# Experts' weights in chunks of 8 KB a partition, a fourth pair of split tiles, and two raw tiles fewer

## The chip, the cores and the metric

The kernel runs on one core of a Trainium2 chip. The metric is device time in microseconds (us), the median of several runs. TensorE (PE) does the matrix products, VectorE (DVE) and ScalarE (ACT) the elementwise work, GpSimd (POOL) the indirect transfers, and SyncE (SP) issues most loads; all of them are queues that work in order and wait for one another by semaphores.

## The reference, cut to what matters

One layer of a latent-token model: a recurrent branch and a neighbourhood-attention branch are merged, then comes an expert-choice mixture of experts, and that is where the change lies. 16 experts take 128 tokens of 1024 each, and every expert has three weight matrices of 2M float32 numbers (8 MB each).

```python
def expert_choice_moe(xn, w_router, w_gate, w_up, w_down):
    ...
    g, idx = lax.top_k(aff.transpose(0, 2, 1), cap)
    xe = xn[bidx, idx]
    hid = jax.nn.silu(jnp.einsum('becd,edf->becf', xe, w_gate)) * jnp.einsum('becd,edf->becf', xe, w_up)
    ye = jnp.einsum('becf,efd->becd', hid, w_down) * g[..., None].astype(xn.dtype)
    return jnp.zeros_like(xn).at[bidx, idx].add(ye)
```

## The kernel before, in words

**Split numbers.** To multiply float32 numbers with little loss, each operand is kept as a high part (a rounded copy, type fp32r) and a low part (the number less its high part). `mm3` (lines 185 to 189) makes one product from three matmuls: high by high (L187), high by low (L188), low by high (L189). In the expert stage the tokens are the stationary operand and the weights the moving one, so L188 is the first matmul of a chunk that needs the low part of the weights.

**The weight stream.** The class `Stream` (lines 67 to 159) brings all weights through the kernel as chunks of 1 MB, 128 partitions by 2048 numbers. A chunk passes three stations. `load` (L83 to L92) takes a free raw tile and has SP issue the transfer (L90). `split` (L101 to L125) takes a free pair of split tiles, has ACT copy the chunk to the high tile (`hi_copy`, L181) and, through `finish` (L94 to L99), has DVE subtract to get the low tile (L98); after that the raw tile is free for a further load. `take` (L141 to L150) hands a chunk to PE: it first gives back the pair of the chunk before, then loads what has a tile, then splits what has a pair. So the copy into a pair that was given back waits until PE has done the last matmul of the chunk that was in it.

**Tiles.** There are two kinds of slots, in deques served first in, first out. Pairs: `w0` and `w1` for the whole kernel, `x0` and `x1` from the merge stage on (L1092). Raw tiles: `ring0`, `ring1`, four `ring2`, five `ring3` and, when the routing is done, `sel` and `ring40`. At the end of the merge stage (L1526 to L1532) the pair `x1` is taken out of the pairs and its two tiles, `x1h` and `x1l`, serve as two raw tiles. The expert stage thus has three pairs and 15 raw tiles.

**Order of the expert stage** (`stage_experts`, L1617 to L1766). There are 24 chunks to an expert, 384 in all. For each of four column blocks `f` of the hidden layer, two chunks of the gate matrix and two of the up matrix (128 rows by 512 columns, four row blocks each, so 2 KB runs in memory); then eight chunks of the down matrix (two blocks of 128 rows by 1024 columns, 4 KB runs). A chunk is twelve matmuls of 512 columns. Among the chunks PE also transposes the hidden layer (`turn_h`, L1704), after chunks 4 and 6 of the down matrix the next expert's tokens (`turn_x`, L1672, followed on ACT by L1679 and L1681 and on DVE by L1682), and it adds up the list of the tokens of the expert after that (`expert_list`, L1641, from `one_hot`, L1631). POOL gathers tokens (L1652) and adds results to memory (L1760), both indirect.

**Start and end.** While the routing is still being computed, L1550 splits the first chunks, as many as there are pairs, but leaves their subtractions for later (`defer=True`). When the list of expert 0 is known, POOL gathers its tokens (L1686) and takes on two loads (L1687), DVE does the three subtractions left over, and SP issues a load after each (L1688 to L1690); then come `turn_x` of expert 0 and `one_hot` of expert 1. In the last expert `ahead` (L1771 to L1787) uses freed raw tiles for the final norm's weight (`fnorm`, issued by ACT) and for the rows of the sum; `stage_final` (L1789) works these off.

```python
            if self.pending:
                lo, x, hi, rslot = self.pending.popleft()
                (engine or self.lo_engine).tensor_sub(lo, x, hi)
                self.free.append(rslot)
...
        if not hold:
            self.release()
        self.held.append(i)
        self.load()
        self.split(most if i in self.parts else max(most, 1))
```

Of the kernel before, what the change touches and what calls it, by code (L numbers as in the profile page):

```python
# [22 lines left out]
D = 1024  # L23
# [5 lines left out]
NEXP = 16  # L29
DEXP = 2048  # L30
# [32 lines left out]
def raw(t, off, dims):  # L63
    return bass.AP(tensor=t.tensor, offset=t.offset + off, ap=dims)
# [109 lines left out]
class Kernel:  # L174
# [68 lines left out]
    def setup(self):  # L243
        nc, c = self.nc, self.const
        I = self.I
        self.par = c.tile([128, NPK], F32, name="par")
        nc.scalar.dma_start(self.par, I["pk"])
        self.ident = c.tile([128, 128], F32, name="ident")
        make_identity(nc, self.ident)
        self.ones = c.tile([128, 1], F32, name="ones")  # L250
        nc.vector.memset(self.ones, 1.0)

        W = []

        def tiled(name, n, split):
            for i in range(n):
                W.append((I[name][i], None, split))

        for i in range(12):
            W.append((I["wqkv"][i], None, True))  # L260
        for i in range(16):
            W.append((I["wrnn"][i], None, True))
        for i in range(8):
            W.append((I["wpr"][i % 4], None, True))
        for h in range(2):
            for i in range(4):
                W.append((I["wpn"][i], None, True))
            for i in range(4):
                W.append((I["wout"][i], None, True))
        self.first_expert = len(W)  # L270
        wg, wu, wd = I["w_exp_gate"], I["w_exp_up"], I["w_exp_down"]
        for e in range(NEXP):
            for f in range(4):
                for w in (wg, wu):
                    for kh in range(2):
                        W.append((raw(w, e * D * DEXP + kh * 4 * 128 * DEXP + f * 512,
                                      [[DEXP, 128], [128 * DEXP, 4], [1, 512]]), (4,), True))
            for f2 in range(8):
                W.append((raw(wd, e * DEXP * D + f2 * 256 * D, [[D, 128], [128 * D, 2], [1, D]]), (2,), True))
        self.S = Stream(self, W)  # L280
        self.S.slots(self.ringp, "ring0", "ring1")
        self.S.part_slots(self.hip, "w0", "w1")
# [786 lines left out]
    def stage_merge(self):  # L1069
        nc, I, S = self.nc, self.I, self.S  # L1070
# [9 lines left out]
        def some(n):  # L1080

            some.at += n
            return room[:, some.at - n:some.at]
# [134 lines left out]
        w = [some(128) for i in range(2)]  # L1218
# [307 lines left out]
        c_mix.__exit__(None, None, None)  # L1526
        ring3, self.c_ring3 = self.open_("ring3", side="right", bufs=1)
        S.release()
        S.pfree.remove((self.hip2, "x1"))
        S.slots(self.hip2, "x1h", "x1l")  # L1530
        S.slots(ring3, *(f"ring3{i}" for i in range(5)))
        S.load()  # L1532
        turn_x(7, 1)
# [83 lines left out]
    def stage_experts(self):  # L1617
        nc, I, S, rt = self.nc, self.I, self.S, self.rt
# [8 lines left out]
        def one_hot(e):  # L1627
            if e >= NEXP:
                return
            hots[e] = oh = rt.tile([128, 8, 128], BF16, name="oh", tag="wide")  # L1630
            nc.vector.tensor_tensor(oh, self.iota[:, None, :].to_broadcast([128, 8, 128]),  # L1631
                                    self.pos[:, :, e, None].to_broadcast([128, 8, 128]), op=ALU.is_equal)
# [23 lines left out]
        def turn_x(e, halves):  # L1656
            if e >= NEXP:
                return
            if 0 in halves:
                xe = X[e]  # L1660
                xh = p.tile([128, 8, 128], F32R, name="xeh", tag="xeh", bufs=1)
                xl = p.tile([128, 8, 128], F32R, name="xel", tag="xel", bufs=1)
                gate = p.tile([128, 1], F32, name="gate", tag="gate", bufs=2)
                nc.vector.tensor_copy(gate, xe[:, D + e:D + e + 1])
                X[e] = xh, xl, gate, xe
            xh, xl, gate, xe = X[e]

            xm = xe[:, :D].rearrange("p (k n) -> p k n", k=8)
            for h in halves:
                pt = ps.tile([128, 4, 128], F32, name="pt", tag="pt", bufs=2)  # L1670
                for k in range(4):
                    nc.tensor.transpose(pt[:, k], xm[:, 4 * h + k], self.ident)  # L1672
                for k in range(4):
                    j = 4 * h + k
                    sh, sc = self.mod2[:, j:j + 1], self.mod2[:, 8 + j:9 + j]
                    if e == 0 and k % 2:
                        nc.vector.tensor_scalar(xm[:, j], pt[:, k], sc, sh, op0=ALU.mult, op1=ALU.add)
                    else:
                        nc.scalar.activation(xm[:, j], pt[:, k], AF.Identity, scale=sc, bias=sh)  # L1679
                hs = slice(4 * h, 4 * h + 4)  # L1680
                nc.scalar.copy(xh[:, hs], xm[:, hs])  # L1681
                nc.vector.tensor_sub(xl[:, hs], xm[:, hs], xh[:, hs])  # L1682
# [5 lines left out]
        for _ in range(3):  # L1688
            S.finish()
            S.load()  # L1690
        turn_x(0, (0, 1))
        one_hot(1)
        S.load()
        S.split()
        for e in range(NEXP):
# [40 lines left out]
            for f2 in range(8):  # L1736
# [5 lines left out]
                for a in range(2):  # L1742
                    f = 2 * f2 + a
# [142 lines left out]
def _col(v):  # L1886

    return np.asarray(v).reshape(-1, 128).T
# [23 lines left out]
    return b.reshape(HEADS, 128, BCOLS)  # L1912


def prep(x, c, ctx, c_ctx, w_mod, b_mod, w_in, b_in, conv_w, conv_b, lru_wa, lru_ba, lru_wi, lru_bi, lru_lambda,
         na_rpb, w_proj_rnn, w_proj_na, w_out, w_router, w_exp_gate, w_exp_up, w_exp_down, final_norm):
    A = lambda t: np.asarray(t)
    w_in, b_in = A(w_in)[0], A(b_in)[0]
    b_mod = A(b_mod)[0]
    off = {n: i * D for i, n in enumerate(("yg", "xr", "q", "k", "v", "gr", "gn"))}  # L1920
    qc, kc = _qk_columns(off["q"]), _qk_columns(off["k"])
    qkv = []
    for g in range(4):
        qkv += [qc[g * 256:(g + 1) * 256], kc[g * 256:(g + 1) * 256],
                np.arange(off["v"] + g * 256, off["v"] + (g + 1) * 256)]
    rnn = []
    for kind, j in LRU_ORDER:
        for n in (("xr", "yg") if kind == "in" else ("gr", "gn")):
            rnn.append(np.arange(off[n] + j * 128, off[n] + (j + 1) * 128))
    pk = {  # L1930
        "c": _col(A(c)[0]), "cctx": _col(A(c_ctx)), "bsh1": _col(b_mod[:D]), "bsc1": _col(b_mod[D:2 * D]),
        "bxr": _col(b_in[off["xr"]:off["xr"] + D]), "byg": _col(b_in[off["yg"]:off["yg"] + D]),
        "bgr": _col(b_in[off["gr"]:off["gr"] + D]), "bgn": _col(b_in[off["gn"]:off["gn"] + D]),
        "bq": _col(b_in[qc]), "bk": _col(b_in[kc]),
        "convw": np.concatenate([_col(A(conv_w)[0, i]) for i in range(4)], 1), "convb": _col(A(conv_b)[0]),
        "lba": np.concatenate([_col(A(lru_ba)[0, d]) for d in range(2)], 1),
        "lbi": np.concatenate([_col(A(lru_bi)[0, d]) for d in range(2)], 1),
        "lam": np.concatenate([_col(A(lru_lambda)[0, d]) for d in range(2)], 1),
        "wr": A(w_router)[0].reshape(8, 128, 16).transpose(1, 0, 2).reshape(128, 128),
    }  # L1940
    packed = np.empty((128, NPK), np.float32)
    for n, (a, b) in _cols.items():
        packed[:, a:b] = pk[n]
    wa = A(lru_wa)[0].reshape(2, 8, 128, 64)
    wi = A(lru_wi)[0].reshape(2, 8, 128, 64)
    lw = np.stack([wa[0], wi[0], wa[1], wi[1]], 2)
    cos, sin = _rope_tables()
    p = np.arange(128)
    same = p[:, None] % 16 == p[None, :] % 16
    tiles = np.stack([same, same & (p[:, None] // 16 < p[None, :] // 16)], 1).astype(np.float32)  # L1950
    return {
        "tiles": tiles, "x": A(x)[0], "ctx": A(ctx)[0], "pk": packed,
        "wm": _chunks(A(w_mod)[0]), "bmod": np.ascontiguousarray(b_mod[2 * D:].reshape(4, D)),
        "wqkv": _chunks(w_in, np.concatenate(qkv)), "wrnn": _chunks(w_in, np.concatenate(rnn)),
        "bv": np.ascontiguousarray(b_in[off["v"]:off["v"] + D].reshape(1, D)),
        "lw": np.ascontiguousarray(lw), "cos": cos, "sin": sin,
        "wpr": _chunks(A(w_proj_rnn)[0]), "wpn": _chunks(A(w_proj_na)[0]), "wout": _chunks(A(w_out)[0]),
        "bias": _bias_rows(A(na_rpb)[0]),
        "w_exp_gate": A(w_exp_gate)[0], "w_exp_up": A(w_exp_up)[0], "w_exp_down": A(w_exp_down)[0],
        "fnorm": A(final_norm).reshape(1, D),  # L1960
    }

# [10 lines left out]
```

## Time and profile before

| | |
|---|---|
| runs, median of 3 | 2628.53 us (2625.5 to 2629.2) |
| the profiled execution's own time | 2631.97 us |
| its span from first to last instruction | 2630.2 us |
| mean granted TensorE clock over the span | 0.978 of full speed |
| busy: PE, DVE, ACT, POOL | 95%, 72%, 58%, 11% of the span |
| moved by the DMA engines | 661.80 MB, 252 GB/s over the span |

All of it comes from one profiled execution. Busy time of PE counts matmuls that overlap in the engine, so a PE that is busy without a break may still start its matmuls late: how it does is seen from the starts of single matmuls. A wait is named by engine and line, `<-` stands for what ended it, and `PEld` is PE's loading of a stationary operand, which waits in front of the matmul that belongs to it. `L98` and `L181` are lines of helpers and so stand for every chunk of the stream.

### The profile page before, as it was taken

Reading aid. Unit: us, or ns where it says so; the run is one execution under the profiler, and the core shown is the slowest. Engines: PE = TensorE matmul, PEld = TensorE weight load, DVE = VectorE, ACT = ScalarE, POOL = GpSimd, SP = SyncE. Lnnn points to the kernel's source line nnn. Section 1 sums busy time; section 2 is a strip of 40 time slices with the busy share of each in tenths; the row PEclk is TensorE's granted clock in tenths of the full one; section 3 lists DMA queues with packets and bytes.
Section 4 is the critical chain, followed back from the end, with each engine's and each line's share of the span. In section 5 each row is a group of like instructions: output and inputs, shape, how many; then the busy total and the mean of one; then the engine's idle time right before and its main releaser. Section 6 shows DMA issues by size and latency. Waiting matters only on the chain.

```text
span 2630.2 us, 34531 instructions
## 1 busy us (share of the span) xinstructions
PE 2490.4 (95%) x13401; PEld 2035.6 (77%) x13401; DVE 1888.0 (72%) x2300; ACT 1535.5 (58%) x1699; POOL 301.9 (11%) x269
## 2 busy tenths in 40 slices
PE   7999999999998799999997799999999999999996
PEld 4888888777886687787986577777777777777775
DVE  5675633655564566666466788888888898888888
ACT  5321125466655556565333577777777777777776
POOL 1321110121120000000120000000000000000001
PEclk9999999999999899999998899999999999999998
DMA  8354441122216959645875799999999999999985
GB/s 274 131 206 169 180 141 36 66 74 86 97 42 202 287 187 291 187 153 211 272 238 202 282 362 367 366 365 364 372 372 370 376 370 366 367 367 367 365 306 226
DMA packets 260148, 661.80 MB, mean 252 GB/s; under 512 B 18001, under 2 KB 35553, under 8 KB 250257
## 3 DMA queue, kind: packets, MB, share of 16 engines
q1 hardware_dynamic: 236768, 585.18, 62.8%
q0 software_dynamic: 15120, 62.21, 7.0%
q10 hardware_dynamic: 8096, 12.21, 1.5%
q8 instruction: 105, 1.72, 0.3%
q14 instruction: 59, 0.48, 0.1%
HBM read 585.02 MB, written 74.53 MB: 251 GB/s over the span
## 4 chain that ended last, share of the span: by engine, by line
PE 72%; DVE 10%; ACT 9%; DMA 5%; issue 3%; SPq 0%; ACTq 0%; POOLq 0%; DVEq 0%
PE pm L188 9%; PE pm L189 9%; PE pm L187 9%; PE po L187 3%; PE po L189 3%; PE po L188 3%; PE pv L949 2%; PE pp L187 2%; PE pp L188 2%; PE pp L189 2%; PE pt L932 2%; PE mm L187 2%; PE mm L189 2%; PE mm L188 2%; DVE w0l L98 2%
## 5 line engine op out<-in xcount | busy, mean ns | idle before, releaser
L98 DVE TENSOR_TENSOR w1l<-ring,w1h 128x2048 fp32r<-128x2048 f32 x150 | 343.3, 2288 | 72.5 <-ACT w1h L181 72.0
L98 DVE TENSOR_TENSOR w0l<-ring,w0h 128x2048 fp32r<-128x2048 f32 x123 | 281.8, 2291 | 81.6 <-ACT w0h L181 81.2
L181 ACT CAST w1h<-ring 128x2048 fp32r<-128x2048 f32 x150 | 286.2, 1908 | 70.8 <-PE pm L189 42.6
L181 ACT CAST w0h<-ring 128x2048 fp32r<-128x2048 f32 (+1 forms) x125 | 236.8, 1895 | 101.2 <-PE pm L189 45.2
L98 DVE TENSOR_TENSOR x0l<-ring,x0h 128x2048 fp32r<-128x2048 f32 x81 | 185.5, 2290 | 34.6 <-ACT x0h L181 34.4
L181 ACT CAST x0h<-ring 128x2048 fp32r<-128x2048 f32 x81 | 154.4, 1906 | 32.3 <-PE pm L189 16.3
L909 DVE CUSTOM_DVE_ANT_0 e<-sp,bias 128x640 f32<-128x640 f32 (+1 forms) x128 | 100.7, 787 | 83.1 <-PE sp L905 73.4
L188 PE MATMUL pm<-w0l,xeh 128*128 128x512 f32 x384 | 154.2, 402 | 2.8 <-DVE w0l L98 2.8
L187 PE MATMUL pm<-w0h,xeh 128*128 128x512 f32 x384 | 154.6, 403 | 1.7 <-ACT xeh L1681 1.7
L189 PE MATMUL pm<-w0h,xel 128*128 128x512 f32 x384 | 152.6, 397 | 0.0
L1760 POOL DMA_INDIRECT d_acc<-y,idx x15 | 50.5, 3366 | 873.0 <-DVE y L1759 873.0
L934 ACT COPY et<-pt 128x640 f32<-128x640 f32 (+1 forms) x128 | 84.7, 662 | 106.6 <-PE pt L932 104.9
L917 ACT ACTIVATE e<-e,mx 128x640 f32<-128x640 f32 (+1 forms) x128 | 103.0, 805 | 43.3 <-DVE mx L911 41.8
L187 PE MATMUL pm<-x0h,xeh 128*128 128x512 f32 x320 | 128.2, 401 | 0.0
L188 PE MATMUL pm<-w1l,xeh 128*128 128x512 f32 x320 | 128.1, 400 | 0.0
L187 PE MATMUL pm<-w1h,xeh 128*128 128x512 f32 x320 | 127.9, 400 | 0.0
L188 PE MATMUL pm<-x0l,xeh 128*128 128x512 f32 x320 | 126.8, 396 | 0.4 <-DVE x0l L98 0.4
L189 PE MATMUL pm<-w1h,xel 128*128 128x512 f32 x320 | 126.8, 396 | 0.0
L189 PE MATMUL pm<-x0h,xel 128*128 128x512 f32 x320 | 126.5, 395 | 0.0
L187 PE MATMUL pp<-xh,w1h 128*128 128x512 f32 (+1 forms) x304 | 116.3, 382 | 3.9 <-ACT tg L730 3.2
L188 PE MATMUL pp<-xl,w1h 128*128 128x512 f32 (+1 forms) x304 | 115.9, 381 | 0.0
L189 PE MATMUL pp<-xh,w1l 128*128 128x512 f32 (+1 forms) x304 | 115.7, 381 | 0.0
(458 smaller groups left out, 6894.0 us busy)
## 6 DMA issues: line engine op xcount, KB each, us to landing
ring<-w_exp_up SPq DMA_DIRECT2D x104, 1024.0 KB
ring<-w_exp_down SPq DMA_DIRECT2D x102, 1024.0 KB
ring<-w_exp_gate SPq DMA_DIRECT2D x100, 1024.0 KB
k<-d_k SPq DMA_DIRECT2D x64, 320.0 KB
wmr<-wm POOLq DMA_DIRECT2D x16, 1024.0 KB, 9.0
ring<-wrnn SPq DMA_DIRECT2D x16, 1024.0 KB
ring<-wqkv SPq DMA_DIRECT2D x12, 1024.0 KB
bias<-bias SPq DMA_DIRECT2D x16, 704.0 KB
```

Of the source, the lines that this page charges most:

```text
L98: (engine or self.lo_engine).tensor_sub(lo, x, hi)
L181: self.nc.scalar.copy(hi, x)
L187: mm(out, wh, xh, start=first, stop=False)
L188: mm(out, wh, xl, start=False, stop=False)
L189: mm(out, wl, xh, start=False, stop=last)
L909: nc.vector.tensor_tensor_reduce(e[:, :w], sp[:, c0:c0 + w], b[:, b0:b0 + w], 1.0, -3.0e38, op0=ALU.add, op1=ALU.max, accum_out=mx[:, 0:1])
L917: nc.scalar.activation(e[:, :w], e[:, :w], AF.Exp, bias=mx[:, 1:2], accum_out=mx[:, 2:3])
L932: nc.tensor.transpose(pt[:, c * 128:(c + 1) * 128], e[:, c * 128:(c + 1) * 128], self.ident)
L934: nc.scalar.copy(et[:, :w], pt[:, :w])
L949: nc.tensor.matmul(pv[j * 64:(j + 1) * 64, (s % 4) * 128:(s % 4 + 1) * 128], v[:, t, j * 64:(j + 1) * 64], state[n - 1 + j][:, c * 128:(c ...
L1760: nc.gpsimd.indirect_dma_start(out=self.d_acc[:, :], out_offset=bass.IndirectOffsetOnAxis(ap=self.idx[:, e:e + 1], axis=0), in_=y[:, :], i ...
```

## The change

The host lays the three expert matrices out anew, so that each chunk is one block of 1 MB in memory in which every partition has its 2048 numbers in one run of 8 KB; the order of the chunks and what stands where in a tile stay the same. The pair `x1` stays a pair in the expert stage, and its two tiles are no raw tiles: four pairs, 13 raw tiles. As L1550 now splits four chunks ahead, a fourth subtraction is left over, and it is done between `turn_x` of expert 0 and `one_hot` of expert 1.

```diff
@@ setup
             for f in range(4):
                 for w in (wg, wu):
                     for kh in range(2):
-                        W.append((raw(w, e * D * DEXP + kh * 4 * 128 * DEXP + f * 512,
-                                      [[DEXP, 128], [128 * DEXP, 4], [1, 512]]), (4,), True))
+                        W.append((w[e, 2 * f + kh], None, True))
             for f2 in range(8):
-                W.append((raw(wd, e * DEXP * D + f2 * 256 * D, [[D, 128], [128 * D, 2], [1, D]]), (2,), True))
+                W.append((wd[e, f2], None, True))
@@ stage_merge
         S.release()
-        S.pfree.remove((self.hip2, "x1"))
-        S.slots(self.hip2, "x1h", "x1l")
         S.slots(ring3, *(f"ring3{i}" for i in range(5)))
         S.load()
@@ stage_experts
         turn_x(0, (0, 1))
+        S.finish()
         one_hot(1)
         S.load()
         S.split()
@@ prep
+def _in_chunks(w):
+    return np.ascontiguousarray(w.reshape(NEXP, 2, 4, 128, 4, 512).transpose(0, 4, 1, 3, 2, 5)).reshape(NEXP, 8, 128, 2048)
+def _out_chunks(w):
+    return np.ascontiguousarray(w.reshape(NEXP, 8, 2, 128, D).transpose(0, 1, 3, 2, 4)).reshape(NEXP, 8, 128, 2048)
...
-        "w_exp_gate": A(w_exp_gate)[0], "w_exp_up": A(w_exp_up)[0], "w_exp_down": A(w_exp_down)[0],
+        "w_exp_gate": _in_chunks(A(w_exp_gate)[0]), "w_exp_up": _in_chunks(A(w_exp_up)[0]),
+        "w_exp_down": _out_chunks(A(w_exp_down)[0]),
```

## Rows read from the trace of the kernel before

**Rows 1.** The page, busy time, share of the span and instructions of each engine.

```profile
PE 2490.4 (95%) x13401; PEld 2035.6 (77%) x13401; DVE 1888.0 (72%) x2300; ACT 1535.5 (58%) x1699; POOL 301.9 (11%) x269
```

**Rows 2.** PEld's waits, 1470 to 2610 us: us in total, times, longest us.

```profile
PEld pm L188 <- DVE w0l L98: 9.3, 15, 0.6
PEld po L188 <- DVE x0l L98: 6.3, 15, 0.4
PEld pm L188 <- DVE w1l L98: 4.1, 15, 0.3
```

**Rows 3.** The chain that ended last, at one change of experts: start us, us, what.

```profile
1890.07 1.51 ACT xe L1679 x4
...
1892.13 1.91 ACT w0h L181
...
1894.07 2.30 DVE w0l L98
...
1896.41 0.50 PE pm L188
1896.91 0.23 PE pm L189
```

**Rows 4.** The timeline of PE at that change of experts: start us, us, instruction.

```profile
1889.79 0.48 PE L187 MATMUL po<-x0h,hh 128*128 128x512 f32 x1
1890.38 0.50 PE L188 MATMUL po<-x0l,hh 128*128 128x512 f32 x1
1890.72 0.40 PE L189 MATMUL po<-x0h,hl 128*128 128x512 f32 x1
...
1895.85 0.39 PE L187 MATMUL pm<-w0h,xeh 128*128 128x512 f32 x1
1896.41 0.50 PE L188 MATMUL pm<-w0l,xeh 128*128 128x512 f32 x1 [0.17 <-DVE w0l L98]
...
1902.13 0.50 PE L188 MATMUL pm<-w1l,xeh 128*128 128x512 f32 x1
1902.47 0.40 PE L189 MATMUL pm<-w1h,xel 128*128 128x512 f32 x1
```

**Rows 5.** The page's costliest groups: one chunk's subtraction on DVE, one copy on ACT.

```profile
L98 DVE TENSOR_TENSOR w1l<-ring,w1h 128x2048 fp32r<-128x2048 f32 x150 | 343.3, 2288 | 72.5 <-ACT w1h L181 72.0
...
L181 ACT CAST w1h<-ring 128x2048 fp32r<-128x2048 f32 x150 | 286.2, 1908 | 70.8 <-PE pm L189 42.6
```

**Rows 6.** Windows: us; busy PE, PEld, DVE, ACT, POOL; granted clock; DMA share; GB/s.

```profile
20.00:26.00 6.00, 5.10 (x13) 1.52 (x14) 4.27 (x10) 3.50 (x5) 0.00 (x0) 0.50 1.01 418
1480.00:2540.00 1060.00, 1055.41 (x4754) 839.32 (x4753) 933.31 (x593) 798.38 (x628) 68.07 (x28) 1.00 1.01 367
```

**Rows 7.** Waits of SP's queue, 1480 to 2540 us (longest row of three alike).

```profile
SPq L90 <- DVE x0l L98: 306.1, 118, 5.0
```

**Rows 8.** The timeline at the start of the expert stage.

```profile
1454.62 2.18 POOL L1652 DMA_INDIRECT xe<-d_xn,idx  x1 [18.88 <-DVE idx L1644]
...
1466.18 0.79 PE L187 MATMUL pm<-w0h,xeh 128*128 128x512 f32 x1 [1.73 <-ACT xeh L1681]
...
1469.40 1.22 DVE L1631 TENSOR_TENSOR oh<-iota,pos 128x1024 bf16<-128x1024 f32 x1
```

**Rows 9.** Line L1652, the gathers of tokens: time from issue to landing.

```profile
DMA to landing us min/median/max: 7.4/8.2/10.4
```

**Rows 10.** The timeline of PE in the last expert.

```profile
2566.70 0.48 PE L187 MATMUL pm<-x0h,xeh 128*128 128x512 f32 x1
2567.55 0.49 PE L188 MATMUL pm<-x0l,xeh 128*128 128x512 f32 x1 [0.36 <-DVE x0l L98]
```

**Rows 11.** Waits of SP's queue, 2400 to 2640 us.

```profile
SPq L90 <- DMA ring<-fnorm: 20.0, 1, 20.0
```

**Rows 12.** The timeline at the end: PE's last matmul, then DVE.

```profile
2607.28 0.40 PE L189 MATMUL po<-w1h,hl 128*128 128x512 f32 x1
...
2608.54 1.40 DVE L1834 SCALAR_TENSOR_TENSOR y<-po,gate,g 128x512 f32<-128x512 f32 x2
```

## The prediction

> **What bounds the kernel now.** I read the page first, for the busiest engine: PE works in 95% of the span [rows 1]. The last matmul of the last expert starts at 2607.28 and the first of expert 0 at 1466.18 [rows 8, 12], so the expert stage takes 1141.5 us for 384 chunks, 2.97 us each. That is the stretch the change is about.
>
> Two things could set that pace, PE or the stream of weights, and the windows seem to say both: in 1480 to 2540 PE is busy in 1055.41 of 1060 us at a granted clock of 1.00, and the DMA engines' share is 1.01 at 367 GB/s [rows 6]. The waits of SP's queue decide it. SP, which issues the loads, waited 306.1 us in 118 waits for DVE's subtraction L98 into the low tile of one pair alone, and two more rows of the kind are as large [rows 7]: the stream waits for raw tiles to come free, and PE for no load anywhere in the stage. PE holds the pace, and a faster transfer by itself is worth nothing.
>
> Next I asked whether PE ever waits. A chunk is 12 matmuls at a step of 0.23 us [rows 3], 2.8 us; the rest of the 2.97 is transposes and lists, apart from three waits at each change of experts. PEld's waits show them: for the low tile of `w0` 15 times, of `x0` 15 times, of `w1` 15 times, always at L188, the first matmul that needs a chunk's low part [rows 2]. The chain of waits tells why [rows 3]. After the second half of `turn_x` ACT must make four pieces of the tokens (1.51 us from 1890.07), so the copy of the next chunk starts only at 1892.13; it takes 1.91, the subtraction 2.30, and PE has stood waiting until 1896.41. The chain leaves PE here once per expert.
>
> The price is in PE's timeline [rows 4]. From L187 at 1889.79 to L188 is 0.59 us instead of 0.23: 0.36 lost; the next step is 0.34: 0.11 lost. At 1895.85 it is 0.56: 0.33 lost, and I take 0.11 again for the step behind it. At 1902.13 the step after the wait is 0.34: 0.11. Together 1.02 us a change of experts.
>
> **The fourth pair.** A copy may begin when PE has left the pair. With three pairs the copy and the subtraction, 1.91 + 2.29 = 4.2 us [rows 5], have two chunks of PE's time, 5.6 us: 1.4 to spare, against a copy that comes some 2.3 us late (PE had left the pair's last chunk by 1889.79, the copy started at 1892.13 [rows 3, 4]). With four pairs they have three chunks, 8.4 us: 4.2 to spare. Two halves of `turn_x`, two chunks apart, add up to less: 2.3, less the 0.5 to 0.9 that DVE and ACT win back on each of two chunks (2.8 against 2.29 and 1.91), plus 2.3 is 2.8 to 3.6. Both queues have the room: DVE is busy in 933 of 1060 us, ACT in 798 [rows 6]. So I take the three waits as gone: 15 changes of experts by 1.02 is 15.3 us. The last expert has one more, where ACT's queue is held by the load of `fnorm`: 0.85 instead of 0.23, 0.62 lost [rows 10], covered too. Sum **-15.9 us**; the floor is no gain at all, should the wait only move. What comes late next is nothing near: all other pairs of matmuls run at PE's own step.
>
> **The layout.** Bytes, number of loads and their order are the same; a chunk is 128 runs of 8 KB instead of 512 of 2 KB or 256 of 4 KB. The trace has such loads: the first weights of the kernel are 8 KB a partition, and they run at 418 GB/s [rows 6], or 1.0486 MB in 2.51 us, against 2.86 at the stage's mean of 367. Cost on the path: nothing, since PE's 2.8 us of matmuls per chunk cover it. It makes room for the shorter stage: at 2.93 us a chunk even 2.86 would just fit.
>
> **Two raw tiles fewer.** A load is issued when a subtraction frees its tile, 13 chunks or 38 us before use instead of 15 or 44. The slowest transfer of the stage that the trace gives a landing for is a gather, 10.4 us [rows 9]. Nothing on the path; 28 us of cover.
>
> **The start.** The fourth copy ahead (1.91) runs on ACT while it waits for the routing. The fourth subtraction (2.29) stands on DVE in front of `one_hot` of expert 1, which moves from 1469.40 to about 1471.7 and ends 1472.9 [rows 8]; PE asks for its list after two chunks, 24 steps of 0.23 after 1466.18, not before 1471.7, and later as the first matmul took 0.79 [rows 8]. I take 0, at worst 1.2. Then the gather of expert 0, which is on the path (issued at 1454.62; PE's first matmul on its tokens at 1466.18 [rows 8]). SP's loads share the DMA engines with it, and their packets become larger. Gathers take 7.4 to 10.4 us, 8.2 in the median [rows 9], and this one, the only one that ends while PE stands, is taken to be at the short end; I take the difference to the median, **+0.8 us**, with 0 and +3 as ends.
>
> **The end.** At PE's last matmul (over at 2607.7) DVE was still at earlier rows of the final norm and came to `y` at 2608.54 [rows 12]. The last copy now comes one chunk earlier, so this work does as well: **-0.8 us**, between 0 and -2.8.
>
> **Sum.** -15.9 + 0.8 - 0.8 = -15.9 us. The profiled execution took 2631.97 with 2630.2 of span, so 2616.1 for it; it lies 3.4 above the median of the runs, 2628.53, from which I forecast 2612.6.
>
> **The rivals.**
> - *The wait moves.* The late copies add up over the two halves of `turn_x` to more than the 4.2 us to spare (my sum reaches 3.6), and half the loss stays: 2620.5. For it speaks how near the sum is; against it, that DVE and ACT still have 12% and 25% of the stage idle.
> - *The stream is the bound.* Then a fourth pair helps nothing: 2628.5. The DMA share of 1.01 speaks for it; the 306 us that SP waited for tiles against it, and the 418 GB/s of 8 KB runs. The Trainium skill ("DMA: Bandwidth & Descriptors", "Where 436 GB/s comes from") has it that loads from HBM are held at about 358 GB/s for a core; by that rule the stage runs at its limit today and the change gives nothing. The trace disagrees: 367 is its mean over 1060 us.
> - *The stock runs dry, slower than before.* Once the stream stands still for long: in the last expert SP waits 20.0 us for `fnorm` to land, with loads still to issue [rows 11]. Before, 15 raw tiles and three pairs carried PE over it, 18 chunks; now 17, or 50 us of PE's work. Less some 10 us for a load, a copy and a subtraction, each us beyond 40 costs one; to eat the gain and be 0.2% slower the wait would have to last 40 + 16 + 5 = 61 us: 2634. Against it: nothing in the change makes this wait three times as long; for it, only that the order of frees and loads changes.
> - *The change does not do what it says*: the fourth pair might never be split ahead because ACT's copies wait in order. The same 2628.5, counted with the second.
>
> **How the numbers follow.** My forecast has 0.80, the moved wait 0.09, no change 0.08, the dry stock 0.03. 0.2%, about what a measurement of this kernel can tell from no change, is 5.3 us. Forecast and moved wait are both faster: 0.89; same 0.08; slower 0.03. The range goes from 2608 (end at -2.8, start at 0, and about 2 us for the runs' own spread of 2625.5 to 2629.2) to 2621 (start at +3 and 1.2, end at 0, or the moved wait at 2620.5).
>
> **What would show it.** Right: PEld's waits at L188 for `w0`, `x0` and `w1` gone, or some tenths of a us in all; the chain stays on PE through the changes of experts; expert to expert 1 us shorter; fewer packets, the mean in GB/s up a little with the DMA share down to about 0.9; PE's first matmul near 1467. Wrong: L188 still waiting behind L1679; a load among what ends PE's or ACT's waits; a first matmul after 1469.

## The result, and the profile after

The kernel after takes 2613.36 us in the median of 4 runs (2612.92 to 2614.25), the kernel before beside it 2628.86: a ratio of 0.9947, 95% interval 0.9933 to 0.9961. The forecast was 2612.6 us, with a range of 2608 to 2621. The profiled execution of after took 2614.25 us with a span of 2612.4, against 2631.97 and 2630.2. Of the runs further below, one execution of six_raw_old took 9933.4 us, and its median and ratio are those of the other five.

Where the 17.8 us between the two spans come from (first and last matmul of the stage as in [rows 8, 12] and in the rows below):

| stretch of the span | before, us | after, us | difference |
|---|---|---|---|
| up to the first matmul of expert 0 | 1466.18 | 1465.13 | -1.05 |
| from it to the start of the last matmul | 1141.10 | 1126.52 | -14.58 |
| from there to the end | 22.91 | 20.74 | -2.18 |

PEld's waits of after, 1470 to 2610 us (us in total, times, longest). The three rows of L188 [rows 2] are gone, and so is the wait of [rows 10]; what is left is the list's wait for `one_hot`, which was there before as well (6.3 us, 14 times):

```profile
PEld L1638 <- DVE oh L1628: 6.5, 14, 0.5
```

PE's timeline at the change of experts of [rows 4]. From the down matrix's last matmuls into the next expert all steps are 0.23, L188 included; the next expert begins at 1960.31, 70.38 us later, where before it was 71.3:

```profile
1889.46 0.40 PE L188 MATMUL po<-w1l,hh 128*128 128x512 f32 x1
1889.70 0.39 PE L189 MATMUL po<-w1h,hl 128*128 128x512 f32 x1
1889.93 0.39 PE L187 MATMUL pm<-w0h,xeh 128*128 128x512 f32 x1
1890.16 0.40 PE L188 MATMUL pm<-w0l,xeh 128*128 128x512 f32 x1
1890.39 0.40 PE L189 MATMUL pm<-w0h,xel 128*128 128x512 f32 x1
...
1960.31 0.39 PE L187 MATMUL pm<-w0h,xeh 128*128 128x512 f32 x1
```

The chain of waits of after stays on PE there, where it left for ACT and DVE before [rows 3]:

```profile
1889.39 0.23 PE po L187
1889.62 0.24 PE po L188
1890.32 0.23 PE pm L188
1890.55 0.24 PE pm L189
```

Over 1480 to 2540 us every line of that chain is now PE's. Before, 8.1% of the stretch lay on ACT and DVE (2.1% on L1679, 2.7% on the copy into `w0`, 3.3% on its subtraction).

How near is the next wait? The timeline shows the tightest chunk of this change: its subtraction ends at 1894.26 + 2.28 = 1896.54, and PE asks for the low part at 1898.57, 2.03 us later. Over the 324 chunks from 1550 to 2500 us no margin is smaller; before, the smallest were 0.05 us, a wait. Directly in front of that subtraction DVE works off `y`, the result of the expert just ended (1.40 us), which the prediction's account of the lateness leaves out; its copy on ACT was over at 1892.11.

```profile
1892.94 1.40 DVE L1757 SCALAR_TENSOR_TENSOR y<-po,gate,g 128x512 f32<-128x512 f32 x2
1894.26 2.28 DVE L98 TENSOR_TENSOR w1l<-ring,w1h 128x2048 fp32r<-128x2048 f32 x1
...
1898.57 0.39 PE L188 MATMUL pm<-w1l,xeh 128*128 128x512 f32 x1
```

The windows of after, columns as in [rows 6]: DMA's share falls from 1.01 to 0.96 while it moves 372 GB/s for 367.

```profile
1480.00:2540.00 1060.00, 1059.58 (x4815) 852.64 (x4814) 945.06 (x601) 806.08 (x633) 71.72 (x29) 1.00 0.96 372
```

SP's queue still waits for raw tiles and not for the stream, 1480 to 2540 us (the longest of four such rows, the shortest of which is 142.4 us; [rows 7] before). In 2400 to 2640 us its wait for `fnorm` is 15.1 us, 20.0 before [rows 11]:

```profile
SPq L90 <- DVE w1l L98: 267.1, 91, 5.0
```

The start of the expert stage in after, to be read beside [rows 8]:

```profile
1453.72 2.18 POOL L1649 DMA_INDIRECT xe<-d_xn,idx  x1 [18.88 <-DVE idx L1641]
...
1461.04 0.15 DVE L1661 COPY gate<-xe 128x1 f32<-128x1 f32 x1 [1.67 <-DMA xe<-d_xn,idx]
...
1465.13 0.79 PE L187 MATMUL pm<-w0h,xeh 128*128 128x512 f32 x1 [1.73 <-ACT xeh L1678]
...
1468.35 2.28 DVE L98 TENSOR_TENSOR w1l<-ring,w1h 128x2048 fp32r<-128x2048 f32 x1
...
1470.55 1.22 DVE L1628 TENSOR_TENSOR oh<-iota,pos 128x1024 bf16<-128x1024 f32 x1
...
1472.93 0.35 PE L1638 MATMUL pt<-tok,oh 128*128 128x2 bf16 x8
```

And the end, beside [rows 12]: DVE now waits for PE and begins `y` 0.43 us after the last matmul's start, not 1.26.

```profile
2591.65 0.40 PE L189 MATMUL po<-w1h,hl 128*128 128x512 f32 x1
2592.08 1.41 DVE L1832 SCALAR_TENSOR_TENSOR y<-po,gate,g 128x512 f32<-128x512 f32 x2 [1.89 <-PE po L189]
...
2592.80 2.36 POOL L1820 TENSOR_TENSOR ring<-ring,ring 128x1024 f32<-128x1024 f32 x1 [0.34 <-ACT ring L1819]
2593.53 2.71 DVE L1833 TENSOR_TENSOR ring<-ring,y 128x1024 f32<-128x1024 f32 x1
...
2598.23 2.34 POOL L1820 TENSOR_TENSOR ring<-ring,ring 128x1024 f32<-128x1024 f32 x1 [3.07 <-ACT ring L1819]
...
2598.47 2.12 DVE L1803 TENSOR_TENSOR small<-small 128x2 f32<-128x2 f32 x1
```

### The profile page after: what moved, and what is told of

Read it like the earlier page. It is cut to its first block, busy times and chain, and to the rows that moved or that the text cites. A ratio compares the mean times of both kernels' runs of the same rounds, so it can differ in the third digit from the quotient of the medians.

```text
span 2612.4 us, 34543 instructions
## 1 busy us (share of the span) xinstructions
PE 2478.6 (95%) x13401; PEld 2038.4 (78%) x13401; DVE 1885.1 (72%) x2300; ACT 1534.0 (59%) x1699; POOL 302.4 (12%) x269
## 4 chain that ended last, share of the span: by engine, by line
PE 76%; DVE 9%; ACT 7%; DMA 5%; issue 2%; ACTq 0%; SPq 0%; POOL 0%; POOLq 0%; DVEq 0%
PE pm L187 9%; PE pm L189 9%; PE pm L188 9%; PE po L187 5%; PE po L189 5%; PE po L188 5%; PE pv L948 2%; PE pp L187 2%; PE pp L188 2%; PE pp L189 2%; PE pt L931 2%; PE mm L187 2%; PE mm L189 2%; PE mm L188 2%; PE pq L187 2%
## 5 line engine op out<-in xcount | busy, mean ns | idle before, releaser
L98 DVE TENSOR_TENSOR w1l<-ring,w1h 128x2048 fp32r<-128x2048 f32 x110 | 251.8, 2289 | 58.8 <-ACT w1h L181 58.8
L181 ACT CAST w1h<-ring 128x2048 fp32r<-128x2048 f32 x110 | 209.8, 1907 | 49.8 <-PE pv L189 23.6
L98 DVE TENSOR_TENSOR x1l<-ring,x1h 128x2048 fp32r<-128x2048 f32 x93 | 212.9, 2290 | 8.1 <-ACT x1h L181 7.0
L181 ACT CAST x1h<-ring 128x2048 fp32r<-128x2048 f32 x93 | 177.3, 1907 | 49.3 <-PE pm L189 31.6
L188 PE MATMUL pp<-xl,w1h 128*128 128x512 f32 (+1 forms) x304 | 115.8, 381 | 0.0
L187 PE MATMUL pp<-xh,w0h 128*128 128x512 f32 (+1 forms) x272 | 107.2, 394 | 4.6 <-ACT tg L729 3.5
L904 PE MATMUL sp<-k,q 128*128 128x256 f32 (+1 forms) x512 | 102.1, 323 | 8.1 <-DVE mx L908 6.5
L931 PE MATMUL pt<-ident,e 128*128 128x128 f32 x608 | 91.1, 279 | 18.7 <-ACT et L933 9.6
L188 PE MATMUL pp<-xl,w0h 128*128 128x512 f32 (+1 forms) x272 | 106.7, 392 | 0.0
L189 PE MATMUL pp<-xh,w0l 128*128 128x512 f32 (+1 forms) x272 | 106.6, 392 | 0.0
L187 PE MATMUL pm<-x1h,xeh 128*128 128x512 f32 x256 | 105.4, 412 | 0.0
```

Of the source, the lines that this page charges most:

```text
L181: self.nc.scalar.copy(hi, x)
L187: mm(out, wh, xh, start=first, stop=False)
L188: mm(out, wh, xl, start=False, stop=False)
L189: mm(out, wl, xh, start=False, stop=last)
L904: nc.tensor.matmul(sp[:, a:a + m], q[:, s * 128:(s + 1) * 128], ks[part][:, k0:k0 + m], start=part == 0, stop=part == 1)
L931: nc.tensor.transpose(pt[:, c * 128:(c + 1) * 128], e[:, c * 128:(c + 1) * 128], self.ident)
```

## The experiments

All twelve kernels in one table. The ratio is to the kernel before, run beside them. "Expert to expert" is the usual distance between the first matmuls of two experts in the profile.

| kernel | median, us | ratio and 95% interval | expert to expert, us |
|---|---|---|---|
| layout_only | 2629.34 | 1.0000, 0.9991 to 1.0009 | 71.3 |
| pairs_only | 2612.04 | 0.9930, 0.9916 to 0.9945 | 70.4 |
| three_pairs_13 | 2628.42 | 0.9999, 0.9989 to 1.0008 | 71.3 |
| six_raw_new | 2613.76 | 0.9937, 0.9924 to 0.9950 | 70.4 |
| six_raw_old | 2611.46 | 0.9929, 0.9916 to 0.9942 | 70.4 |
| five_pairs | 2606.32 | 0.9910, 0.9897 to 0.9924 | 70.2 |
| pairs_wyz | 2601.89 | 0.9897, 0.9882 to 0.9912 | 69.9 |
| pairs_xyz | 2604.26 | 0.9904, 0.9889 to 0.9920 | 69.9 |
| oh_early | 2609.78 | 0.9921, 0.9908 to 0.9934 | 70.2 |
| five_oh | 2605.41 | 0.9906, 0.9892 to 0.9920 | 70.0 |
| tail_dve | 2610.65 | 0.9924, 0.9910 to 0.9937 | 70.4 |
| all_three | 2598.13 | 0.9882, 0.9866 to 0.9899 | 69.7 |

One caution for reading it: the first matmul of the expert stage starts anywhere between 1458.68 (all_three) and 1466.18 (before) in these profiles, though the code that runs up to the end of the merge stage is the same in all. Differences of a few us between medians are therefore read from the stage itself.

### The change taken apart

The layout alone, three pairs and 15 raw tiles:

```diff
+        S.pfree.remove((self.hip2, "x1"))
+        S.slots(self.hip2, "x1h", "x1l")
...
         turn_x(0, (0, 1))
-        S.finish()
         one_hot(1)
```

> The new layout of the experts' weights alone, with three pairs and 15 raw tiles as in the kernel before. Theory (PE waits for split weights, never for raw tiles): the time stays at the 2628.9 us of before, within 0.2%; the three L188 waits of 0.36, 0.11 and 0.33 us at each change of experts are still there, expert to expert 71.3 us; only the DMA share of the expert stage falls, and the bytes per us of a full-speed stretch rise. Rival (the stream is the bound, and the layout is what was gained): 2613 to 2616 us with three pairs still in place.

The four pairs and 13 raw tiles alone, an edit of the kernel before, with the weights as they lay there:

```diff
-        S.pfree.remove((self.hip2, "x1"))
-        S.slots(self.hip2, "x1h", "x1l")
...
         turn_x(0, (0, 1))
+        S.finish()
         one_hot(1)
```

> The old layout with the fourth pair and 13 raw tiles, and the extra finish() ahead of one_hot(1). Theory (the fourth pair is the whole gain): about 2613.4 us, 0.5 to 0.7% under before, no wait at L188 at a change of experts, expert to expert 70.4 us. Rival (the stream is the bound): 2626 to 2630 us, with the waits moved to a raw tile that has not landed. Between the two, 2617 to 2624 us, would say that the pair brings the gain only where a faster stream refills the two tiles fewer.

The kernel before without the two raw tiles:

```diff
         S.pfree.remove((self.hip2, "x1"))
-        S.slots(self.hip2, "x1h", "x1l")
```

> The kernel before with two raw tiles fewer and nothing else: old layout, three pairs, 13 raw tiles. Theory (15 tiles were more than the stalls of the queue need): 2628.9 us within 0.2%, expert to expert 71.3 us. Rival (the raw tiles taken are a cost that the layout pays back): slower, 2632 to 2640 us, with PE or ACT waiting for a landing behind the gather or the fnorm wait.

The windows and the L188 waits of layout_only, then the windows of pairs_only:

```profile
1480.00:2540.00 1060.00, 1055.29 (x4753) 839.20 (x4752) 933.30 (x593) 798.08 (x627) 74.79 (x28) 1.00 0.96 367
```

```profile
PEld pm L188 <- DVE w0l L98: 9.4, 15, 0.6
PEld po L188 <- DVE x0l L98: 6.3, 15, 0.4
...
PEld pm L188 <- DVE w1l L98: 4.1, 15, 0.3
```

```profile
1480.00:2540.00 1060.00, 1059.55 (x4814) 852.63 (x4814) 945.02 (x601) 806.20 (x633) 81.07 (x29) 1.00 1.02 372
```

The theory holds in all three. The layout lowers the DMA share from 1.01 to 0.96 and leaves the time, the rate and the waits as they were [rows 2, 6]. The pairs alone bring the whole gain, with DMA engines busy all the time and 372 GB/s out of runs of 2 and 4 KB. The two raw tiles cost nothing.

### How much stock the stream needs

I expected the layout to be a reserve that a short stock would draw on, and took seven raw tiles away, in both layouts:

```diff
-        S.slots(ring3, *(f"ring3{i}" for i in range(5)))
...
-        S.slots(self.sel, "sel")
...
-        S.slots(p, "ring40")
```

> The kernel after with 6 raw tiles in place of 13 (the five ring3 tiles, sel and ring40 are not given to the stream); four pairs, new layout. In the traces a chunk of the kernel after has landed at least 22 us before ACT splits it, with 15 tiles 30 us: some 3 us per tile, so 6 tiles leave about 1 to 2 us. Theory (the stock is far from dry, the stream is no bound): 2612 to 2617 us, expert to expert 70.4 to 70.6 us. Rival (13 tiles are about as few as the queue's stalls allow): 2625 us or more, ACT waiting for landings at each change of experts.

> The same 6 raw tiles and four pairs with the old layout. Here a chunk takes longer to land (median 8.6 us from issue against 7.4) and DMA is busy all the time, so it can make up a delay only slowly. Theory (the layout is a reserve that only a short stock draws on): 2616 to 2640 us, slower than with the new layout by 3 us or more, ACT waiting for landings behind each gather and scatter. Rival (the layout is worth nothing at any stock): within 0.1% of six_raw_new.

```profile
1480.00:2540.00 1060.00, 1059.51 (x4817) 852.65 (x4815) 945.34 (x600) 806.01 (x634) 82.94 (x29) 1.00 1.02 372
```

That row is six_raw_old. Six tiles are enough in either layout, and my expectation for the old one was a miss. From a chunk's last transfer record to its copy on ACT, the trace has, between experts 1 and 14, at least 22 us in after, 1.4 us in six_raw_new and 0.6 in six_raw_old: the old layout does bring the stock nearer to nothing, but not there, and PE's rows are the same. The rival won: the layout is worth nothing even at six tiles.

### A fifth pair, and what it turned up

```diff
-        S.slots(ring3, *(f"ring3{i}" for i in range(5)))
+        S.part_slots(ring3, "y")
+        S.slots(ring3, *(f"ring3{i}" for i in range(3)))
...
-        S.split(4, defer=True)
+        S.split(5, defer=True)
...
         one_hot(1)
+        S.finish()
```

> The kernel after with a fifth pair made of two of the ring3 tiles, so 11 raw tiles, and one more deferred subtraction, behind one_hot(1). Theory (with four pairs PE waits for no split weight any more): nothing more is gained, 2612 to 2615 us, expert to expert 70.4 us, the one_hot wait of some 0.2 us per expert untouched. Rival (the fourth pair only pushed the waits along, each pair more takes as much again): 2600 to 2606 us. Rival (11 raw tiles are too few for the stalls of the queue): 2618 us or more.

It was 2606.32, outside of the theory's numbers, at the edge of the first rival's, but not by that rival's way: the waits are the same row as in after (6.5 us for `one_hot`), and the margin that was 2.03 us is 4.75, so no wait was left to remove. By the profiles the span is 7.3 us shorter than that of after: 1.9 of it lie ahead of the stage, 3.9 in the stage and 1.5 behind PE's last matmul, where a GpSimd multiplication is over before DVE's addition begins (see "The end"). What differs in the stage is PE's own step. Taken from the starts of consecutive matmuls, 1500 to 2500 us, it is 233.6 ns in after and 232.8 here (steps over 300 ns, where a transpose or a list lies between, left out), and by tiles only the fifth pair stands out: 229 ns in the first two GEMMs (gate and up), the tiles of the other four pairs 231 to 236, each of the three matmuls taken by itself. With five pairs every pair passes through all places in the order of the chunks, so it is not that order. So I moved two of four pairs to the same pool, ring3:

```diff
-        S.slots(ring3, *(f"ring3{i}" for i in range(5)))
+        for i in range(2):
+            S.pfree.remove((self.hip2, f"x{i}"))
+            S.slots(self.hip2, f"x{i}h", f"x{i}l")
+        S.part_slots(ring3, "y", "z")
+        S.slots(ring3, "ring30")
```

> Four pairs and 13 raw tiles as in the kernel after, but two of the pairs lie in ring3 (y, z) in place of x0 and x1, whose four tiles become raw ones. With five pairs the chunks that lay in the fifth pair ran the first GEMMs at 229 ns per matmul, all others at 232 to 235 ns. Theory (the place of the split weights in SBUF sets this pace): y and z chunks at 229 ns, w chunks at 233 to 234, some 0.4 us less per expert, 70.0 us from expert to expert, 2605 to 2609 us. Rival (the rotation by five, which writes go on beside the reads, or the number of pairs made it): all chunks at 233 to 234 ns, 70.4 us, 2612 to 2615 us.

> The same with w0 and w1 turned into raw tiles, and x0, x1, y and z as the four pairs. Theory of the place: as the run before, y and z chunks at 229 ns, x chunks at 233 to 234 ns, 2605 to 2609 us. Rival: 2612 to 2615 us. If only one of the two kernels is faster, it is the distance to what is written beside it and not the place alone.

PE's timeline in pairs_wyz, the first matmul of five chunks in a row:

```profile
1953.21 0.39 PE L187 MATMUL pm<-w0h,xeh 128*128 128x512 f32 x1
...
1956.02 0.39 PE L187 MATMUL pm<-w1h,xeh 128*128 128x512 f32 x1
...
1958.83 0.39 PE L187 MATMUL pm<-yh,xeh 128*128 128x512 f32 x1
...
1961.57 0.39 PE L187 MATMUL pm<-zh,xeh 128*128 128x512 f32 x1
...
1964.29 0.40 PE L187 MATMUL pm<-w0h,xeh 128*128 128x512 f32 x1
```

A chunk in `w0` or `w1` takes 2.81 us, in `y` 2.74, in `z` 2.72, at a granted clock of 1.00 and with no wait between them. Both kernels gain, whichever old pairs are left: their stage is 8.9 and 8.5 us shorter than that of after. So it is where the weights lie that sets the step, and no count of pairs. Both medians lie below the theory's range, because `z` ran faster than the 229 ns expected; of pairs_wyz's a further 2.9 us lie ahead of the stage. In the down matrix's chunks `y` and `z` run at 233 ns like all others. What it is about the place (the address itself, or what lies or is written beside it), and why `z` is faster than `y`, stays open; it was not tried further.

### The wait that is left

```diff
+            one_hot(e + 2)
             for f2 in range(8):
...
                     turn_h(3)
-                    one_hot(e + 2)
```

> The kernel after with one_hot(e + 2) moved from the second chunk of the third GEMM to a point before its first chunk. Theory (the list's matmul waits for one_hot on DVE, 0.2 us net for each of 14 experts, and that is the last wait of the expert stage): 2.6 us less than after, 2609 to 2612 us, expert to expert 70.2 us, the L1628 wait gone, no L188 wait in its place. Rival (DVE has no room, the 1.2 us come back as a wait for a subtraction): 2613 to 2616 us with L188 waits for the third or fourth chunk.

> Five pairs with 11 raw tiles (2606.3 us measured, against 2612 to 2615 expected) and one_hot early. Theory: the two add up, 2603 to 2605 us, expert to expert 70.0 us. Rival (five pairs already cover what the early one_hot brings): 2606 to 2607 us.

(five_oh is five_pairs with this edit.)

The timeline of after, then that of oh_early (DVE's `one_hot`, PEld's wait for it):

```profile
1873.49 1.22 DVE L1628 TENSOR_TENSOR oh<-iota,pos 128x1024 bf16<-128x1024 f32 x1
1874.76 0.27 PEld L1638 LDWEIGHTS <-oh 128*128 128x128 bf16 x8 [0.46 <-DVE oh L1628]
```

```profile
1872.19 0.27 PEld L1638 LDWEIGHTS <-oh 128*128 128x128 bf16 x8 [0.28 <-issue]
```

0.46 of wait becomes 0.28 for which the profile names no cause: 0.18 us an expert, as the 70.20 us from expert to expert say against 70.38. On the fifth pair it saves the same, 70.2 to 70.0, though the median, 2605.41, fell between the theory's range and the rival's; with an interval that overlaps that of five_pairs, it decides nothing. DVE takes the move without a new wait.

### The end

```diff
         def aside(i, a):
-            x = self.tails[i][:, a]
-            nc.scalar.activation(x, x, AF.Identity, scale=ys[i][:, a:a + 1])
-            nc.gpsimd.tensor_mul(x, x, self.fn)
-            store(i, a)
+            scaled(i, a)
```

> The kernel after with the three multiplications of the last norm that GpSimd did given to DVE (no ACT scaling and no GpSimd tensor_mul: one DVE instruction of 1.28 us for each). In the kernel after DVE's L1833 took 2.71 us and one L1803 2.12 us while a GpSimd multiplication ran, against 0.16 us for the other L1803. Theory (a DVE instruction that meets a running GpSimd multiplication does not end before it): L1833 at 1.2 to 1.4 us, all small ones at 0.15 to 0.17 us; DVE gets 3.8 us of work more, of which 1.3 us fits into its wait for PE and 2.7 to 3.2 us are saved: the time from the last matmul to the end changes by less than 1 us, 2612 to 2614 us. Rival (the long ones wait for ACT or for PSUM, not for GpSimd): L1833 stays at 2.7 us, and the end comes 2.5 us later, 2616 us.

```profile
2591.91 1.23 DVE L1830 TENSOR_TENSOR ring<-ring,y 128x1024 f32<-128x1024 f32 x1
...
2596.44 0.16 DVE L1803 TENSOR_TENSOR small<-small 128x2 f32<-128x2 f32 x1
```

The instructions that took 2.71 and 2.12 us take 1.23 and 0.16 without GpSimd beside them: the theory's mechanism. The effect was larger than its "less than 1 us": from the last matmul's start at 2590.03 to the end of the span at 2609.24 it is 19.2 us, against 20.7. five_pairs and five_oh end in 19.2 us as well, without this edit: there GpSimd's second multiplication ends before the addition begins, and the addition takes 1.22 us.

### A version that beats both

pairs_wyz with the edits of oh_early and tail_dve.

> The three edits that were faster than the kernel after, together: two of the four pairs in ring3 (pairs_wyz, 2601.9 us), one_hot early (2.6 us less by the 0.18 us per expert of oh_early), the last norm without GpSimd (1.5 us less from the last matmul to the end by the profile of tail_dve). Theory (three separate places, so they add up): 2596 to 2600 us, expert to expert 69.7 us, last matmul to end 19 to 19.5 us. Rival (with faster matmuls DVE becomes the bound of the expert stage, its subtractions of 2.2 us and the one_hot no longer fit): 2600 to 2604 us, with L188 waits back.

2598.13 us, 1.2% under the kernel before and 0.6% under the kernel after; 69.67 us from expert to expert, 19.2 us from the last matmul to the end, no L188 wait. The three add up: the stage is 11.4 us shorter than that of after and the end 1.5, where the three kernels by themselves gave 11.9 and 1.5. A further 6.4 us of its profile lie ahead of the stage, where none of the edits was aimed.

## Why the prediction was right

- **PE holds the pace, the stream doesn't.** Shown by layout_only (no change) and pairs_only (the whole gain). The Trainium skill ("DMA: Bandwidth & Descriptors", "Where 436 GB/s comes from") has loads from HBM held at about 358 GB/s for a core, which it works out as half of what a stack gives its two cores; by that a shorter stage was not to be had. The trace disagrees, with 372 GB/s over 1060 us in either layout, but by less than this number or the prediction's 367 says: some 7 GB/s of it are results added to memory (0.52 MB an expert), so by this estimate loads alone are about 364 now and 360 before. Clearer are the loads into free tiles as the stage begins, 424 GB/s in after (last section); here one core runs alone.
- **The fourth pair, -15.9.** The stage gave -14.6. From expert to expert it is 0.94 less, 14 times, where the waits made 1.02; of the difference 0.015 is in the list's wait (6.3 to 6.5 in 14), the rest I did not locate. The last expert gave 1.22, of which my terms explain 1.17: 0.62 for `fnorm` and 0.33, 0.11 and 0.11 for the two waits at its start. The first gave only 0.15 of the 0.47 that its end had: PE began earlier, while its steps were still 0.43 us (granted clock 0.50, the lower level, from 1465.2 to 1469.4, after a stand of 9.1 us for the gather), and made ten steps at that pace instead of nine, 0.2 us; the rest I did not locate.
- **The moved wait** (0.09) was further off than my sum of 2.8 to 3.6 us late against 4.2 said: the tightest margin is 2.03, not 0.6 to 1.4. The number came out safe, but the sum behind it was not the right one: it added ACT's pieces up and left out `y` on DVE, behind which the tightest chunk stands. Before, the third wait (`w1` at 1902.13) stood behind `y` as well, and not behind ACT alone: DVE worked on it for 1.40 us from 1898.48, right ahead of that subtraction.
- **The layout and the raw tiles, 0 and 0.** Both right. The cover was smaller than the 28 us I gave, at least 22 us between experts 1 and 14 and 15 in the last one, but with seven tiles less again 0.6 us is still enough. DMA's share fell to 0.96 and not to about 0.9.
- **The start, +0.8.** Wrong in size, inside the ends: DVE read the gather's tokens 1461.04 - 1453.72 = 7.3 us after its issue, 7.5 by the same reading before, so in this one execution of each the larger packets beside it cost nothing. That PE begins 1.05 earlier is mostly the 0.9 by which the gather is issued earlier, ahead of the change. The fourth subtraction ran at 1468.35, `one_hot` ended at 1471.77, and the list at 1472.93 followed without a wait: 0, as taken.
- **The end, -0.8.** It was -2.2. My part is there to the digit, 1.26 to 0.43. The rest is DVE and GpSimd meeting in other places: before, two short DVE instructions were held up beside a GpSimd multiplication, after only one (2.12), for 2.15 less; the addition into `mine` (the rows of the last expert's tokens) went from 1.94 to 2.71, for 0.77 more. The kernel before:

```profile
2609.98 1.94 DVE L1835 TENSOR_TENSOR ring<-ring,y 128x1024 f32<-128x1024 f32 x1
2611.22 2.91 POOL L1822 TENSOR_TENSOR ring<-ring,ring 128x1024 f32<-128x1024 f32 x1 [0.38 <-ACT ring L1821]
2611.84 2.31 DVE L1803 TENSOR_SCALAR small<-small 128x2 f32<-128x2 f32 x1
...
2616.30 2.12 DVE L1805 TENSOR_TENSOR small<-small 128x2 f32<-128x2 f32 x1
```

- **What I passed over.** I wrote that apart from the L188 waits all steps were PE's own. The wait for `one_hot` stood in the same view (6.3 us, 14 times), worth 2.5 us as oh_early shows, and PE's own step was not a constant.

The forecast lay within 1 us of the median. The mechanism is shown; that closeness is in part luck. The profiles are 17.7 us apart and the medians 15.5, and single runs of the kernel before lie anywhere from 2624.2 to 2633.3. By the profiles the stage gave 1.3 us less than forecast, and the start and the end 1.9 and 1.4 more.

## What to carry to other kernels

When a slot is refilled by a chain of engines (copy, subtraction), count how late the chain can come and how many slots' time it has; here the tightest margin went from a wait to 2.0 us with the fourth pair and to 4.75 with the fifth, and once the waits were gone more margin brought nothing: what the fifth pair gained in the stage came from PE's step. DMA engines that are busy all the time are no proof that the stream is the bound: ask what the issuing queue waits for. And read PE's step tile by tile before calling it a constant.

## What was not expected of the hardware

**The place of the moving operand.** By the mean distance of starts (pairs_wyz, 1500 to 2500 us) the same matmul steps at 226.7 ns with its weights in `z`, at 229 in `y` and at 234 in `w0` and `w1`, up to 3% apart, in the first two GEMMs alone; putting two of four pairs there is worth 0.53 us an expert.

**DVE and GpSimd hold each other up.** A DVE instruction on 128x2 numbers takes 2.31 us when it meets a GpSimd multiplication and ends with it (2611.84 + 2.31 against 2611.22 + 2.91); GpSimd is held too: that multiplication, begun while DVE's addition ran (until 2611.92), took 2.91 us, one of after, begun with no such neighbour, 2.34. Not all of DVE's work waits: a reciprocal at 2598.28 in after took 0.16 beside the multiplication of 2598.23, and the two instructions of [rows 12] at 2608.54, which read PSUM, took 0.74 each inside one that ran from 2607.64 to 2610.84. The Trainium skill ("SBUF — State Buffer", "SBUF: two separate sides") describes a pair of ports that the two share and that one of them holds for its whole instruction, and the trace agrees.

**Run length.** At PE's demand of 372 GB/s, runs of 2 and 4 KB kept up for 1060 us as well as runs of 8 KB did; the difference shows in the DMA share alone, 1.02 for 0.96. Beyond that demand there is one stretch, as the stage begins and free tiles are filled: there the runs of 8 KB move 424 GB/s and, in the kernel before, runs of 4 KB 399. So a DMA share of 1.01 at 367 GB/s [rows 6] was not the most that the stream could give. The windows of before, then of after, columns as in [rows 6]:

```profile
1462.00:1470.00 8.00, 5.76 (x17) 4.58 (x18) 3.60 (x8) 2.96 (x6) 0.00 (x0) 0.50 1.03 399
```

```profile
1462.00:1470.00 8.00, 6.27 (x19) 4.82 (x18) 4.50 (x7) 2.97 (x6) 0.00 (x0) 0.52 1.01 424
```
